# Two layers in one TensorE-bound kernel: gains of the key and first query weights applied in place, and another order of the last steps

## The chip, the cores and the metric

The kernel runs on one core of one Trainium2 chip. The metric is the device time of one execution in microseconds (us), the median over several runs. The engines are named as in the profile: PE is TensorE's matmul, PEld its weight load, DVE is VectorE, ACT is ScalarE, POOL is GpSimd, and SP issues most transfers.

## The reference

One step of an encoder with two layers on 1024 prompt rows and 32 rows of a running stream (1056 columns in all), width 1024. The first layer is a gated linear recurrence, the second an attention over a window of key and value rows that are computed once between the layers. All of it is float32.

```python
def shared_kv(h, norm_kv, w_kv, pos):
    kv = rmsnorm(h, norm_kv) @ w_kv
    k = rope(kv[..., :kvw].reshape(B, T, N_KV_HEADS, HEAD_DIM), pos)
    v = kv[..., kvw:].reshape(B, T, N_KV_HEADS, HEAD_DIM)
...
def swa_block(x, pos, norm_pre, w_in, sinks, w_out, norm_post, k, v, attend):
    u = rmsnorm(x, norm_pre) @ w_in
    q = rope(u[..., :qw].reshape(B, T, N_HEADS, HEAD_DIM), pos)
    o = attend(q, k, v, sinks)
    y = (o * jax.nn.silu(u[..., qw:])) @ w_out
    return x + rmsnorm(y, norm_post)
```

`rmsnorm(x, g)` is x / sqrt(mean(x^2) + 1e-6) * g.

## The kernel before

Each float32 product is three matmuls: both factors are split into a high part (`hi`, rounded to the format that TensorE reads) and a low part (`lo`, the rest), and hi*hi, hi*lo and lo*hi are summed (`mm3`, `mm3_steps`). Weights come in half tiles of 128 rows by 4 x 128 columns (`weights`, L135): a load into `raw`, the gain of the norm, and the split into `whi` and `wlo`. The pools behind these names are rings: `raw` has four slots, `whi` and `wlo` six each, and a load or a write waits until a slot is free. The raw tiles of kA lie in a pool of their own with two slots (L141). For most second-layer weights POOL multiplies the gain into `raw` (L147), ACT copies it to `hi` (L128) and DVE subtracts (L129). For the names in `GAIN_ACT` (kA, kB, qA0, qB0: the two halves of the key weights and of the first query weights) the gain is taken up in the split itself, column block by column block (`split_scaled`, L131 to L133): four scaled copies on ACT and four scale-and-subtract steps on DVE for each half tile.

The rest around them: the value weights (`prep_v`, L849) also go through `split_scaled`, but the change leaves them as they are. Between the layers lies what is called the seam here. For each of three column blocks n of 384, 384 and 288 columns, the first layer's output is normed and added to the input (`post_norm`, L660 and L666), split to `xh` and `xl`, squared on ACT (L673, tile `qx`), summed on POOL (L675) and reduced by a matmul with a matrix of ones (L188, tile `ss_x`). The key matmuls rAk and rBk, the value matmuls vc (L167 to L169) and their transposition (L839, after a scaling on DVE, L827) run between these steps. `raw_g` names the gate weights of the second layer, which follow the first query weights in the ring.

The order in which each engine takes its instructions is not written down by hand. A scheduler goes through the whole program with its own estimates of durations and takes, on each engine, the ready instruction with the highest rank. The rank is the place in the program; `urgent()` moves it ahead by 300 places, and `pin` keeps an instruction behind those that precede it in the program. On the chip, each engine and each queue then works strictly in that order.

At the end (`out_t`, L1169) the last 256 prompt rows are computed with rows on the partitions: two tiles t of 128 rows, two halves c of 512 columns. ACT squares a finished bank and sums it along the row (L1200), DVE multiplies it by the gain (L1203) into `zt`. When both halves of a tile are there, 1/sqrt is taken from ACT's approximation y and refined once by r = y * (1.5 - 0.5 * m * y * y), with m the mean square; then z * r plus the residual (L1215) goes out in two stores of 512 columns (L1216). The last half of the last tile is computed in two parts of 256 columns, each with its own sum (s2 and s1).

Of the kernel before, what the change touches and what calls it, by code (L numbers as in the profile page):

```python
# [11 lines left out]
AF = mybir.ActivationFunctionType  # L12
ALU = mybir.AluOpType
# [62 lines left out]
def _trunk(ctx, tc, nc, A):  # L76
    V, S, G = nc.vector, nc.scalar, nc.gpsimd
# [10 lines left out]
    def urgent(offset=300):  # L88
        return tc.high_priority(offset=offset)

    def pin(i, on=True):
        return tc.keep_in_program_order(i) if on else i

    def bank(name, tag="mm", bufs=None):
        return psum.tile([P, 512], F32, tag=tag, name=name, bufs=bufs or nbank)
# [24 lines left out]
    def g_of(which, k):  # L120
        return gains[:, which * KD + k:which * KD + k + 1]


    def split(dst_hi, dst_lo, src, lo_eng=None, hi_dve=False, behind=False):
        if hi_dve:
            V.tensor_copy(dst_hi, src)
        else:
            pin(S.activation(dst_hi, src, AF.Copy), behind)  # L128
        (lo_eng or V).tensor_tensor(dst_lo, src, dst_hi.bitcast(F32), op=ALU.subtract)  # L129

    def split_scaled(dst_hi, dst_lo, src, gain, behind=False):  # L131
        pin(S.activation(dst_hi, src, AF.Copy, scale=gain), behind)
        V.scalar_tensor_tensor(dst_lo, src, gain, dst_hi.bitcast(F32), op0=ALU.mult, op1=ALU.subtract)  # L133

    def weights(src, kn, name, gain=None):  # L135

        out = []
        for k0 in range(0, kn, 4):
            kk = min(4, kn - k0)
            if name == "kA":  # L140
                raw = late.tile([P, 4, P], F32, tag="raw", bufs=2, name=f"raw_{name}_{k0}")  # L141
            else:
                raw = ring.tile([P, 4, P], F32, tag="raw", bufs=4, name=f"raw_{name}_{k0}")
            nc.sync.dma_start(raw[:, :kk, :], src[:, k0:k0 + kk, :])
            if gain is not None and name not in GAIN_ACT:
                with urgent():
                    pin(G.tensor_tensor(raw[:, :kk, :], raw[:, :kk, :],  # L147
                                        gains[:, gain * KD + k0:gain * KD + k0 + kk].unsqueeze(2).to_broadcast([P, kk, P]),
                                        op=ALU.mult), name in ("qA1", "qB1"))
            hi = ring.tile([P, 4, P], F32R, tag="whi", bufs=6, name=f"whi_{name}_{k0}")  # L150
            lo = ring.tile([P, 4, P], F32R, tag="wlo", bufs=6, name=f"wlo_{name}_{k0}")
            with urgent():
                if name in GAIN_ACT:
                    for i in range(kk):
                        split_scaled(hi[:, i, :], lo[:, i, :], raw[:, i, :], g_of(gain, k0 + i))
                else:
                    split(hi[:, :kk, :], lo[:, :kk, :], raw[:, :kk, :], G if name in LO_POOL else None, name in HI_DVE)
            out += [(hi[:, i, :], lo[:, i, :]) for i in range(kk)]
        return out
# [468 lines left out]
    def tmp(name, w=384):  # L628
        return late.tile([P, 384], F32, tag="t", bufs=NT, name=name)[:, :w]
# [81 lines left out]
    for n, order in enumerate(orders):  # L711
        zs, acc = {}, []
        w = NSB[n][1] - NSB[n][0]
        for i, m in enumerate(order):
# [5 lines left out]
            ps = bank(f"oa{m}_{n}")[:, :w]  # L720
            mm3(ps, [ws[k] for k in korder], [yhl[k, n] for k in korder])
            z = tmp(f"z{m}_{n}") if n < 2 else late.tile([P, 288], F32, tag="z", bufs=KD, name=f"z{m}_{n}")
# [30 lines left out]
    def mm3_steps(ps, ws, xs, every=6):  # L753
        n, c = len(ws), 0
        for i, ((wh, wl), (xh, xl)) in enumerate(zip(ws, xs)):
            for l, r in ((wh, xh), (wh, xl), (wl, xh)):
                nc.tensor.matmul(ps, l, r, start=c == 0, stop=c == 3 * n - 1)  # L757
                c += 1
                if c % every == 0 and c < 3 * n:
                    yield  # L760
# [311 lines left out]
    def load_og(m, n):  # L1072
        w = width(OUT[n])
        oghl[m, n] = (part(f"ogh{m}_{n}", w), part(f"ogl{m}_{n}", w))
        if m < 6:
            raw = unit(f"ogr{m}_{n}", w=w)
            load_parts(raw, ogscr[m], OUT[n])
            split(*oghl[m, n], raw)
            return
        o = 0  # L1080
        for c0, c1 in OUT[n]:
            i = min(c0 // 384, 2)
            split(*(x[:, o:o + c1 - c0] for x in oghl[m, n]), ogl[m, i][:, c0 - NSB[i][0]:c1 - NSB[i][0]], behind=n == 2 and m == 6)
            o += c1 - c0
# [69 lines left out]
    def fin_tile(name, w, tag, dt=F32, bufs=1):  # L1154
        return fin.tile([P, w], dt, tag=tag, bufs=bufs, name=name)[:, :w]

    def prep_t(c, k):

        raw = ring.tile([P, 4, P], F32, tag="raw", bufs=4, name=f"raw_t{c}_{k}").rearrange("p a b -> p (a b)")
        nc.sync.dma_start(raw, A["w_out_t"][c, k])  # L1160
        if c and k < 6:
            wt[c, k] = tuple(ring.tile([P, 4, P], F32R, tag=f"w{x}", bufs=6, name=f"wt{x}{c}_{k}").rearrange("p a b -> p (a b)")
                             for x in ("hi", "lo"))
        else:
            wt[c, k] = tuple(fin_tile(f"wt{x}{c}_{k}", 512, "wt" + x, F32R, 10) for x in "hl")

        split(*wt[c, k], raw, behind=c == 1)

    def out_t():  # L1169

        gpost = fin_tile("gpost", 1024, "gpost", bufs=1)
        nc.sync.dma_start(gpost, A["gpost"])
        x1t = fin.tile([P, KD, 256], F32, name="x1t")
        nc.sync.dma_start(x1t, x1scr.rearrange("m p c -> p m c")[:, :, 768:SEQ])
        sm = fin.tile([P, 2, 8], F32, name="smt")
        for m in range(KD):
            if (m, 2) not in oghl:
                load_og(m, 2)
        for k in (6, 7, 0, 1, 2, 3, 4, 5):
            prep_t(1, k)  # L1180
        zt = [fin_tile(f"zt{t}", 1024, "zt", bufs=2) for t in range(2)]
        xt = {}

        def residual(t):
            for c in range(2):
                xt[t, c] = bank(f"xt{t}_{c}", "ST"[t], 2)
                for i in range(4):
                    nc.tensor.transpose(xt[t, c][:, i * P:(i + 1) * P], x1t[:, 4 * c + i, t * P:(t + 1) * P], ident)

        for c in range(2):  # L1190
            for t in range(2):
                s0, s1, ms, y, r, s2 = (sm[:, t, i:i + 1] for i in range(6))

                parts = [(0, 256, s2), (256, 512, s1)] if c and t else [(0, 512, s1 if c else s0)]
                for a, b, acc in parts:
                    ps = bank(f"ot{t}_{c}_{a}")[:, :b - a]
                    yield from mm3_steps(ps, [tuple(x[:, t * P:(t + 1) * P] for x in oghl[k, 2]) for k in range(KD)],
                                         [tuple(x[:, a:b] for x in wt[c, k]) for k in range(KD)])
                    junk = fin_tile(f"junk{t}_{c}_{a}", b - a, "junk", bufs=1)
                    S.activation(junk, ps, AF.Square, accum_out=acc)  # L1200
                    if c == 0:
                        V.tensor_scalar(s0, s0, 1.0 / 1024.0, EPS, op0=ALU.mult, op1=ALU.add)
                    V.tensor_tensor(zt[t][:, c * 512 + a:c * 512 + b], ps, gpost[:, c * 512 + a:c * 512 + b], op=ALU.mult)  # L1203
                    if acc is s2:
                        V.scalar_tensor_tensor(s0, s2, 1.0 / 1024.0, s0, op0=ALU.mult, op1=ALU.add)
                if c == 1:
                    residual(t)
                    S.activation(y, s1, AF.Abs_reciprocal_sqrt, bias=s0, scale=1.0 / 1024.0)
                    V.tensor_scalar(ms, s1, 1.0 / 1024.0, s0, op0=ALU.mult, op1=ALU.add)
                    V.tensor_scalar(ms, ms, y, y, op0=ALU.mult, op1=ALU.mult)  # L1210
                    V.tensor_scalar(ms, ms, -0.5, 1.5, op0=ALU.mult, op1=ALU.add)
                    V.tensor_tensor(r, ms, y, op=ALU.mult)
                    for i in range(2):
                        z = zt[t][:, i * 512:(i + 1) * 512]
                        V.scalar_tensor_tensor(z, z, r, xt[t, i], op0=ALU.mult, op1=ALU.add)  # L1215
                        (nc.scalar if i else nc.sync).dma_start(A["o_yt"][t][:, i * 512:(i + 1) * 512], z)  # L1216
                yield

    nb = norm_b(0)
# [7 lines left out]
    for i, _ in enumerate(out_t()):  # L1227
        if i:
            next(nb, None)
# [90 lines left out]
```

## Time and profile before

| | |
|---|---|
| median of 3 runs | 898.28 us (897.15 to 898.77) |
| the profiled execution | 896.39 us, its span 894.6 us |
| PE busy in the span | 881.0 us (98%) |
| DVE busy | 702.3 us (79%) |
| ACT busy | 563.6 us (63%) |
| POOL busy | 211.5 us (24%) |

The span runs from the first to the last instruction of the profiled execution; its own time is 1.8 us longer. All times in rows are counted from the span's start. In rows of a timeline the first number is the start, the second the length; "x4" marks four instructions merged into one row; brackets give the idle time of the engine just before it and what ended it. Names such as `wlo_qA<-raw_qA` give the output and the inputs, and buffer numbers are left out.

### The profile page before, as it was taken

Reading aid. Unit: us, or ns where it says so; the run is one execution under the profiler, and the core shown is the slowest. Engines: PE = TensorE matmul, PEld = TensorE weight load, DVE = VectorE, ACT = ScalarE, POOL = GpSimd, SP = SyncE. Lnnn points to the kernel's source line nnn. Section 1 sums busy time; section 2 is a strip of 40 time slices with the busy share of each in tenths; the row PEclk is TensorE's granted clock in tenths of the full one; section 3 lists DMA queues with packets and bytes.
Section 4 is the critical chain, followed back from the end, with each engine's and each line's share of the span. In section 5 each row is a group of like instructions: output and inputs, shape, how many; then the busy total and the mean of one; then the engine's idle time right before and its main releaser. Section 6 shows DMA issues by size and latency. Waiting matters only on the chain.

```text
span 894.6 us, 15865 instructions
## 1 busy us (share of the span) xinstructions
PE 881.0 (98%) x5462; PEld 863.1 (96%) x5462; DVE 702.3 (79%) x1511; ACT 563.6 (63%) x1233; POOL 211.5 (24%) x257
## 2 busy tenths in 40 slices
PE   9999999999999999999998999999999999999996
PEld 8999999999999999999997999999999999999996
DVE  5877878879897654176889847879999999898777
ACT  7848878789354325355675317756767767797652
POOL 5260212134300001124343532113023011002240
PEclk9999999999999999999999999999999999999999
DMA  9533433352544226446455568336448338444984
GB/s 335 199 107 108 118 100 120 110 147 86 182 128 126 91 55 209 136 133 202 145 171 175 190 183 231 97 101 192 115 125 228 99 120 233 118 135 123 300 259 170
DMA packets 96129, 138.76 MB, mean 155 GB/s; under 512 B 16224, under 2 KB 64128, under 8 KB 96048
## 3 DMA queue, kind: packets, MB, share of 16 engines
q1 hardware_dynamic: 86232, 124.24, 45.6%
q10 hardware_dynamic: 9640, 12.96, 4.8%
q8 instruction: 43, 0.70, 0.3%
q0 software_dynamic: 176, 0.54, 0.2%
q14 instruction: 38, 0.31, 0.1%
HBM read 99.54 MB, written 32.13 MB: 147 GB/s over the span
## 4 chain that ended last, share of the span: by engine, by line
PE 66%; DVE 4%; ACT 2%; DMA 2%; issue 1%; POOL 1%; SPq 0%; DVEq 0%; ACTq 0%; POOLq 0%
PE gB L757 10%; PE rAq L757 5%; PE rBq L757 5%; PE obm L757 5%; PE oa L168 5%; PE oa L167 5%; PE oa L169 5%; PE gb L167 4%; PE gb L168 4%; PE gb L169 4%; PE S L984 3%; PE O L1019 3%; PE T L1009 3%; PE ot L757 2%; PE rAk L757 1%
## 5 line engine op out<-in xcount | busy, mean ns | idle before, releaser
L167 PE MATMUL oa<-yh,whi_outa 128*128 128x384 f32 (+1 forms) x264 | 85.8, 326 | 0.0
L168 PE MATMUL gb<-xlo,whi_ina 128*128 128x384 f32 (+1 forms) x264 | 85.6, 324 | 0.0
L167 PE MATMUL gb<-xhi,whi_ina 128*128 128x384 f32 (+1 forms) x264 | 85.3, 323 | 0.1
L169 PE MATMUL gb<-xhi,wlo_ina 128*128 128x384 f32 (+1 forms) x264 | 85.4, 323 | 0.0
L169 PE MATMUL oa<-yh,wlo_outa 128*128 128x384 f32 (+1 forms) x264 | 85.2, 323 | 0.0
L168 PE MATMUL oa<-yl,whi_outa 128*128 128x384 f32 (+1 forms) x264 | 85.1, 323 | 0.0
L675 POOL TENSOR_TENSOR qp<-qp,qp 128x384 f32<-128x384 f32 (+2 forms) x34 | 42.2, 1242 | 178.5 <-ACT qp L673 166.4
L168 PE MATMUL br<-xlo,whi_ina 128*128 128x384 f32 (+1 forms) x240 | 77.7, 324 | 0.0
L167 PE MATMUL br<-xhi,whi_ina 128*128 128x384 f32 (+1 forms) x240 | 77.7, 324 | 0.0
L169 PE MATMUL br<-xhi,wlo_ina 128*128 128x384 f32 (+1 forms) x240 | 77.5, 323 | 0.0
L129 DVE TENSOR_TENSOR wlo_outa<-raw_outa,whi_outa 128x512 fp32r<-128x512 f32 (+1 forms) x60 | 43.0, 731 | 43.1 <-ACT whi_outa L128 42.9
L989 ACT ACTIVATE P<-P,sm 128x257 f32<-128x257 f32 (+1 forms) x132 | 64.3, 489 | 13.1 <-DVE sm L986 12.8
L757 PE MATMUL gB<-xl,whi_g 128*128 128x384 f32 (+1 forms) x192 | 63.1, 329 | 0.0
L757 PE MATMUL gB<-xh,whi_g 128*128 128x384 f32 (+1 forms) x192 | 63.1, 329 | 0.0
L128 ACT ACTIVATE whi_outa<-raw_outa 128x512 fp32r<-128x512 f32 (+1 forms) x60 | 35.5, 594 | 43.4 <-PE oa L168 23.9
L757 PE MATMUL gB<-xh,wlo_g 128*128 128x384 f32 (+1 forms) x192 | 62.8, 327 | 0.0
L986 DVE CUSTOM_DVE_ANT_0 P<-S,mask,nsnk 128x256 f32<-128x256 f32 (+1 forms) x128 | 53.1, 461 | 5.5 <-PE S L984 5.4
L257 DVE SCALAR_TENSOR_TENSOR conv<-ext,pa,conv 128x1060 f32<-128x1060 f32 (+2 forms) x51 | 46.1, 926 | 11.0 <-ACT conv L255 10.5
L167 PEld LDWEIGHTS gb<-xhi,whi_ina 128*128 128x128 f32 x264 | 49.7, 188 | 0.4 <-DVE u L565 0.4
L167 PEld LDWEIGHTS oa<-yh,whi_outa 128*128 128x128 f32 x264 | 49.6, 188 | 0.4
L168 PEld LDWEIGHTS oa<-yl,whi_outa 128*128 128x128 f32 x264 | 49.6, 188 | 0.4
L169 PEld LDWEIGHTS oa<-yh,wlo_outa 128*128 128x128 f32 x264 | 49.7, 188 | 0.0
(316 smaller groups left out, 2889.4 us busy)
## 6 DMA issues: line engine op xcount, KB each, us to landing
raw_ina<-w_in_a SPq DMA_DIRECT2D x44, 256.0 KB, 3.6
raw_outa<-w_out_a SPq DMA_DIRECT2D x40, 256.0 KB, 3.1
raw_ob<-w_out_b SPq DMA_DIRECT2D x32, 256.0 KB, 3.2
qscr<-quadq SPq DMA_DIRECT2D x8, 768.0 KB
Q<-qscr SPq DMA_DIRECT2D x32, 192.0 KB, 3.8
hscr<-u SPq DMA_DIRECT2D x11, 530.0 KB, 2.7
xr<-xr SPq DMA_DIRECT2D x8, 512.0 KB, 8.9
raw_g<-w_in_b SPq DMA_DIRECT2D x16, 256.0 KB, 5.2
```

Of the source, the lines that this page charges most:

```text
L128: pin(S.activation(dst_hi, src, AF.Copy), behind)
L129: (lo_eng or V).tensor_tensor(dst_lo, src, dst_hi.bitcast(F32), op=ALU.subtract)
L167: pin(nc.tensor.matmul(ps, wh, xh, start=i == 0, stop=False), behind and i == 0 or mid and i == n // 2)
L168: nc.tensor.matmul(ps, wh, xl, start=False, stop=False)
L169: nc.tensor.matmul(ps, wl, xh, start=False, stop=last and i == n - 1)
L257: V.scalar_tensor_tensor(c, e[:, c0 + k:c1 + k], pa[:, t, k:k + 1], c, op0=ALU.mult, op1=ALU.add)
L675: G.tensor_tensor(sums[0], sums[0], q, op=ALU.add)
L757: nc.tensor.matmul(ps, l, r, start=c == 0, stop=c == 3 * n - 1)
L984: pin(nc.tensor.matmul(s, q, KU[g, n][:, hl, ks], start=hl == 0, stop=hl == 1), g == 0 and j == 0)
L986: V.tensor_tensor_reduce(pt[:, h, :w], sb[:, (h - h0) * 256:(h - h0) * 256 + w], msk, -0.125, nsnk[:, sk][:, h:h + 1], op0=ALU.add, op1=AL ...
L989: S.activation(pt[:, h, :w + 1], pt[:, h, :w + 1], AF.Exp, bias=nmax[:, h:h + 1], scale=-1.0, accum_out=rsum[:, h:h + 1])
L1009: nc.tensor.transpose(tb[:, h * P:(h + 1) * P], st["P"][:, h, kt * P:(kt + 1) * P], ident)
```

## The change

For the four weights in `GAIN_ACT`, ACT now multiplies the gain into `raw` in place, four column blocks one by one, and the half tile is then split whole: one copy on ACT, one subtraction on DVE. In `out_t` the refinement is regrouped as r = 1.5 y + (-0.5 m) y * y, so that one small step on DVE goes away, 1.5 y is computed on ACT, and -0.5 times the part of m that is known earlier (s2h) is prepared ahead. The approximation y and the step for m now stand ahead of the last gain multiplication, which is pinned behind them. The last tile's second half is finished and stored in two pieces of 256 columns instead of one of 512; the issue alternates between SP and ACT.

```diff
                 if name in GAIN_ACT:
                     for i in range(kk):
-                        split_scaled(hi[:, i, :], lo[:, i, :], raw[:, i, :], g_of(gain, k0 + i))
+                        S.activation(raw[:, i, :], raw[:, i, :], AF.Copy, scale=g_of(gain, k0 + i))
+                    split(hi[:, :kk, :], lo[:, :kk, :], raw[:, :kk, :])
...
-                s0, s1, ms, y, r, s2 = (sm[:, t, i:i + 1] for i in range(6))
+                s0, s1, ms, y, r, s2, s2h = (sm[:, t, i:i + 1] for i in range(7))
...
-                    V.tensor_tensor(zt[t][:, c * 512 + a:c * 512 + b], ps, gpost[:, c * 512 + a:c * 512 + b], op=ALU.mult)
+                    if acc is s1:
+                        S.activation(y, s1, AF.Abs_reciprocal_sqrt, bias=s0, scale=1.0 / 1024.0)
+                        V.tensor_scalar(ms, s1, -0.5 / 1024.0, s2h, op0=ALU.mult, op1=ALU.add)
+                        S.activation(r, y, AF.Copy, scale=1.5)
+                    pin(V.tensor_tensor(zt[t][:, c * 512 + a:c * 512 + b], ps, gpost[:, c * 512 + a:c * 512 + b], op=ALU.mult), acc is s1)
                     if acc is s2:
                         V.scalar_tensor_tensor(s0, s2, 1.0 / 1024.0, s0, op0=ALU.mult, op1=ALU.add)
+                    if acc is s2 or c == 0:
+                        V.tensor_scalar(s2h, s0, -0.5, None, op0=ALU.mult)
                 if c == 1:
                     residual(t)
-                    S.activation(y, s1, AF.Abs_reciprocal_sqrt, bias=s0, scale=1.0 / 1024.0)
-                    V.tensor_scalar(ms, s1, 1.0 / 1024.0, s0, op0=ALU.mult, op1=ALU.add)
                     V.tensor_scalar(ms, ms, y, y, op0=ALU.mult, op1=ALU.mult)
-                    V.tensor_scalar(ms, ms, -0.5, 1.5, op0=ALU.mult, op1=ALU.add)
-                    V.tensor_tensor(r, ms, y, op=ALU.mult)
-                    for i in range(2):
-                        z = zt[t][:, i * 512:(i + 1) * 512]
-                        V.scalar_tensor_tensor(z, z, r, xt[t, i], op0=ALU.mult, op1=ALU.add)
-                        (nc.scalar if i else nc.sync).dma_start(A["o_yt"][t][:, i * 512:(i + 1) * 512], z)
+                    V.scalar_tensor_tensor(r, ms, y, r, op0=ALU.mult, op1=ALU.add)
+                    for i, (a, b) in enumerate(((0, 512), (512, 768), (768, 1024)) if t else ((0, 512), (512, 1024))):
+                        z = zt[t][:, a:b]
+                        V.scalar_tensor_tensor(z, z, r, xt[t, a // 512][:, a % 512:a % 512 + b - a], op0=ALU.mult, op1=ALU.add)
+                        (nc.scalar if i % 2 else nc.sync).dma_start(A["o_yt"][t][:, a:b], z)
```

## The prediction

> **What bounds the kernel now.** I read the page first (span, engines), then PE's waits, the busy time by stretches around the longest wait, the timeline of each engine there, and at last the chain that ended last.
>
> ```profile
> span 894.6 us, 15865 instructions
> PE 881.0 (98%) x5462; PEld 863.1 (96%) x5462; DVE 702.3 (79%) x1511; ACT 563.6 (63%) x1233; POOL 211.5 (24%) x257
> ```
>
> TensorE is busy 881.0 of 894.6 us, so 13.6 us are not covered by it. The change removes no matmul; it can only touch that remainder and the slow clock behind a pause. Two places matter: the seam between the two layers (460 to 490 us), where the key and first query weights are split, and the end.
>
> ```profile
> 460.00:475.00 15.00, 14.31 (x76) 12.90 (x75) 11.81 (x35) 12.55 (x38) 1.83 (x2) 1.00 0.52 153
> 475.00:480.00 5.00, 4.65 (x25) 4.32 (x25) 4.67 (x11) 0.94 (x2) 0.65 (x1) 1.00 0.88 270
> 480.00:483.00 3.00, 0.05 (x1) 0.05 (x1) 3.00 (x3) 0.00 (x0) 2.90 (x3) 1.00 0.52 121
> 483.00:487.00 4.00, 4.00 (x12) 3.40 (x13) 4.00 (x12) 2.91 (x8) 0.00 (x0) 0.57 0.80 225
> ```
>
> Columns: length, PE, PEld, DVE, ACT, POOL, granted clock, DMA share, GB/s. PE stands still for 0.69 + 0.35 + 2.95 = 4.0 us in the seam, and then four microseconds run at a granted clock of 0.57. VectorE is full from 480 to 487. Who ends the pause:
>
> ```profile
> 472.49 1.26 ACT L132 ACTIVATE whi_qA<-raw_qA,gains 128x128 fp32r<-128x128 f32 x4
> 473.42 1.13 DVE L133 SCALAR_TENSOR_TENSOR wlo_qA<-raw_qA,gains,whi_qA 128x128 fp32r<-128x128 f32 x4
> 474.58 0.87 SPq L144 DMA_DIRECT2D raw_g<-w_in_b  x2
> 474.87 0.55 DVE L660 TENSOR_TENSOR z<-z,r 128x384 f32<-128x384 f32 x1
> 476.47 0.51 ACT L673 ACTIVATE qx<-z 128x384 f32<-128x384 f32 x1
> 479.35 2.38 POOL L147 TENSOR_TENSOR raw_g<-raw_g,gains 128x512 f32<-128x512 f32 x2 [7.26 <-DMA res<-xT]
> 481.69 1.20 POOL L675 TENSOR_TENSOR qx<-qx,qx 128x384 f32<-128x384 f32 x1
> 482.95 1.50 PE L188 MATMUL ss_x<-qx,ones 128*128 128x384 f32 x2 [3.30 <-POOL qx L675]
> ```
>
> The wait of 3.30 us is on GpSimd's sum of squares (L675). Its input qx is there at 476.98, but two gain multiplications of raw_g stand ahead of it on POOL. They start when raw_g lands; raw_g is issued at 474.58, and the last wlo_qA ends at 473.42 + 1.13 = 474.55. So I read the slot of raw_g as freed by the query split: **when the query's lower halves end decides when PE goes on.**
>
> **The change, part by part. Weights.** Eight half tiles (kA, kB, qA0, qB0, two each) of 128x512. Durations in ns (min/median/max):
>
> ```profile
> L132 ACT ACTIVATE whi_kA<-raw_kA,gains x8: 386/388/399, 456.5 to 461.6; 128x128 fp32r<-128x128 f32 x8
> L133 DVE SCALAR_TENSOR_TENSOR wlo_kA<-raw_kA,gains,whi_kA x8: 340/343/1102, 458.1 to 462.1; 128x128 fp32r<-128x128 f32 x8
> L128 ACT ACTIVATE whi_qA<-raw_qA x6: 616/628/635, 539.5 to 676.6; 128x512 fp32r<-128x512 f32 x6
> L129 DVE TENSOR_TENSOR wlo_qA<-raw_qA,whi_qA x6: 675/688/1227, 540.2 to 679.3; 128x512 fp32r<-128x512 f32 x6
> L144 SPq DMA_DIRECT2D raw_kA<-w_k x2: 426/428/430, 331.1 to 331.6; - x2
> ```
>
> Each half now takes four scales on ACT (taken at the 388 ns of the scaled copy of the same shape), one whole copy (628) and one subtraction on DVE (688). ACT gains one copy per half: 0.63 us, of which about 0.1 overlaps its neighbour (four copies of 388 take 1.27 in the rows, not 1.55), so 0.53; over eight halves +4.2 us. DVE gives back 1.13 - 0.69 = 0.44 per half, 3.5 us in all.
>
> What counts is where the scales stand. Before, the scaled copy writes a whi slot (six of them, freed by matmuls). After, it writes raw itself and needs only raw. raw_kA was issued at 331.6, yet its first reader comes at 456.48, so something other than its data holds it, and the slot is the likeliest. Rows of the next stretch:
>
> ```profile
> 456.48 1.27 ACT L132 ACTIVATE whi_kA<-raw_kA,gains 128x128 fp32r<-128x128 f32 x4
> 460.32 0.51 ACT L132 ACTIVATE wh_v<-raw_v,gains 128x256 fp32r<-128x256 f32 x1 [2.57 <-DMA raw_v<-wv]
> 460.73 1.27 ACT L132 ACTIVATE whi_kA<-raw_kA,gains 128x128 fp32r<-128x128 f32 x4
> 462.02 0.34 PE L757 MATMUL rAk<-xh,whi_kA 128*128 128x384 f32 x1
> 465.38 1.12 DVE L133 SCALAR_TENSOR_TENSOR wlo_kB<-raw_kB,gains,whi_kB 128x128 fp32r<-128x128 f32 x4
> 466.53 0.80 SPq L144 DMA_DIRECT2D raw_qA<-w_in_b  x2
> 470.18 0.40 ACT L132 ACTIVATE whi_qA<-raw_qA,gains 128x128 fp32r<-128x128 f32 x1 [1.67 <-DMA raw_qA<-w_in_b]
> ```
>
> ACT idles 2.57 us ahead of 460.32, in which the scales of kB fit (8 x 0.29 = 2.3), and those of kA can go far earlier. I take it that the scheduler places them so. Then each half past 460 costs ACT 0.53 instead of 1.17: for kA's second half and both of kB 3 x 0.64 = 1.9 us less. kB's last lower half ends 1.9 sooner, at 464.6, and raw_qA is issued right behind it (466.53 against 466.50 now) and arrives 1.9 sooner, since 470.18 is a wait for that load. PE's demand at 462.02 is met: the copy of kA's second half starts at 460.72 and ends at 461.35.
>
> The query halves hide nothing, because ACT waits for their load: the first half's copy adds 0.53 and the second's copy and subtraction together 0.5 over the present 0.80 from last copy to last subtraction. I take +0.9 (DVE, lighter, returns 0.1). So raw_g goes out 1.9 - 0.9 = 1.0 us sooner, and L147, L675 and ss_x with it: **-1.0 us**. Bounds: 0, if the scales gain nothing on ACT; -1.9, if the query's extra work hides too. The load of qB0 also meets lighter splits, but its splits stand at 504 us with PE covered; I cost them at nothing, and 2 x 0.53 of ACT time if that cover is gone.
>
> Does the pause's end carry through? PE next needs VectorE here:
>
> ```profile
> 488.68 1.01 DVE L827 TENSOR_TENSOR vc<-vc,r 128x384 f32<-128x384 f32 x2
> 489.49 0.27 PE L839 MATMUL v<-ident,vc 128*128 128x128 f32 x1
> ```
>
> The first vc is ready near 489.2, 0.3 ahead of its transposition. DVE must therefore move up too. Its full stretch begins with L660 at 474.87, right behind the query and value splits, and moves with them by the same 1.0.
>
> **The end.** The last chain, engine by engine:
>
> ```profile
> 888.24 0.19 ACT L1200 ACTIVATION_READ_ACCUMULATOR junk<-ot 128x1 f32 x1
> 888.46 0.42 DVE L1203 TENSOR_TENSOR zt<-ot,gpost 128x256 f32<-128x256 f32 x1 [0.18 <-ACT junk L1200]
> 888.80 0.20 DVE L1209 TENSOR_SCALAR smt<-smt 128x1 f32<-128x1 f32 x1
> 889.11 0.27 DVE L1210 TENSOR_SCALAR smt<-smt 128x1 f32<-128x1 f32 x1
> 889.42 0.15 DVE L1211 TENSOR_SCALAR smt<-smt 128x1 f32<-128x1 f32 x1
> 889.61 0.16 DVE L1212 TENSOR_TENSOR smt<-smt 128x1 f32<-128x1 f32 x1
> 889.87 1.40 DVE L1215 SCALAR_TENSOR_TENSOR zt<-zt,smt,xt 128x512 f32<-128x512 f32 x2
> 890.64 0.33 SPq L1216 DMA_DIRECT2D o_yt<-zt  x1
> 891.50:891.75 0.25, 0.00 (x0) 0.00 (x0) 0.00 (x0) 0.00 (x0) 0.00 (x0) 1.00 0.98 369
> 892.75:893.00 0.25, 0.00 (x0) 0.00 (x0) 0.00 (x0) 0.00 (x0) 0.00 (x0) 0.50 0.52 189
> ```
>
> After: L1209's successor goes first (888.46), zt 0.12 later (888.58), the two squarings by y 0.34 later (888.92, y long there), the last small step 0.31 later (889.23), L1215 0.26 later: 889.49 instead of 889.87, **-0.4 us**. The 1.5 y on ACT runs beside zt. The second half of the row becomes two pieces: half of 1.40, then two 256-wide steps at L1203's pace (0.34 to the next, 0.42 to its end) make 1.46, about as now. The stores run at full DMA share from before 891.5 until 892.9 (512 KB at 369 GB/s is 1.4 us), so they end when the first starts plus 1.4: smaller last stores give nothing of their own. The bounds are 0 (pieces of 1 KB a row move slower and eat it) and -0.7 (the last store's issue counted). The added s2h step (0.15) and the third issue lie off the chain.
>
> Sum: -1.0 - 0.4 = -1.4 us, on the profiled execution's 896.39 us, which is 1.9 under the median of the runs; put on the median it makes 898.28 - 1.4 = 896.9. The short PE waits before 475 (0.69 us) gain nothing, because the pause behind them ends when POOL is done.
>
> **The rivals.** First, the clock. In the 4 us at 0.57, (1 - 0.57) x 4 = 1.7 us were lost after a pause of 3.3. A shorter pause may not bring the clock down. PE would then be 1.7 ahead, but vc on DVE leaves it only the 0.3 us: 896.6. Against it: value matmuls end sooner as well, so the pause may stay near 3. The Trainium skill, TensorE: Matmul & The Clock Gate, "HAM oscillation — how this bites in real kernels", warns of PE gaps over about 3.4 us; the trace agrees about in size, 3.3 us, and by this rule any shortening would keep the clock.
>
> Second, POOL takes qx ahead of raw_g, since qx comes sooner and raw_g's splits stretch. Then DVE decides:
>
> ```profile
> 478.06 5.52 DVE L660 TENSOR_TENSOR z<-z,r 128x288 f32<-128x288 f32 x8
> 483.50 1.92 DVE L666 TENSOR_TENSOR z<-z,res 128x288 f32<-128x288 f32 x5
> ```
>
> Eight at 1.92/5 = 0.38 would be 3.1 us, but took 5.5 while POOL multiplied raw_g. Without that overlap DVE gains up to 2.4 more; I take 1.8: 896.9 - 1.8 = 895.1.
>
> Third, the other side: the scales are not placed ahead but stay where the scaled copies stand. Then kA's second half and both of kB cost 0.53 more each (+1.6), and the query +1.0: raw_g 2.6 later, PE too, less 0.4 at the end: +2.2, 900.5. It decides if the scales of kB stand behind 460.32 on ACT. For it speaks that the scheduler works by its own times, against it the free raw_kA and the 2.57 us.
>
> Fourth, and rarer, scaling qB0 in place as soon as it lands puts a wait for a load ahead of the norm's steps in ACT's queue; up to 3 us if its load lands that much behind them: near 900.
>
> **How the numbers follow.** Main case 0.48 (895.8 to 898.2), clock 0.13, POOL order 0.16, scales not ahead 0.13, qB0 in the way 0.06, anything else 0.04 (both sides). About 0.2% (1.8 us) is what a measurement of this kernel can tell from no change; the main case ends just inside that line, so a quarter of it counts as faster, with half of the clock case and all of the POOL case: 0.12 + 0.07 + 0.16 and an allowance of 0.05 for deeper placement, 0.40; slower 0.13 + 0.06 and 0.01, 0.20; the same 0.40. The range 894.0 to 900.2 leaves out the far end of the POOL case and about half of the slow ones.
>
> **What would show it.** Right: eight scales of kA well ahead of 456 us, kB's ahead of the first wh_v, whole copies of 0.63 behind; raw_qA issued near 464.6; raw_g near 473.6; ss_x near 482; the last tile's first residual step 1.25 us behind the start of its accumulator read (888.24) instead of 1.63. Wrong: scales standing beside the copies at 460 to 467, PE waiting in rAk or rBk, another order on POOL, or a new pause past 490 us from a different plan.

## The result and the profile after

The changed kernel needs 904.49 us (median of 5 runs, 903.28 to 907.07), the kernel before 898.77 (5 runs, 897.15 to 900.01). The ratio is 1.008, 95% interval 1.0061 to 1.010: it is slower by 0.8%, where 896.9 with a range of 894.0 to 900.2 was forecast. The profiled execution of the changed kernel took 904.49 us with a span of 902.7; that of the kernel before had 894.6. From L156 on, line numbers are one higher than before. The page's first lines:

```profile
span 902.7 us, 15871 instructions
PE 884.2 (98%) x5462; PEld 865.3 (96%) x5462; DVE 700.5 (78%) x1489; ACT 569.0 (63%) x1243; POOL 215.4 (24%) x257
```

The same 5462 matmuls keep PE busy for 3.2 us more (884.2 against 881.0), and the span is 8.1 longer. So some matmuls ran slower, and there is about 5 us of new idle time. PE's waits (us in total, times, longest):

```profile
PE v L840 <- DVE vc L828: 4.5, 1, 4.5
PE vc L168 <- ACT wh_v L132: 1.9, 2, 1.2
...
PE rAq L758 <- DVE vc L828: 0.8, 1, 0.8
...
PE ss_x L189 <- POOL qx L676: 0.3, 1, 0.3
```

The pause ahead of ss_x went from 3.3 to 0.3 us, but only because PE comes there later: it has waited 1.9 us for the value weights (wh_v), and behind these waits, of 1.21 and 0.72 us, the granted clock falls to 0.50 for about three microseconds. The row below is the stretch 475 to 480 (length, PE, PEld, DVE, ACT, POOL, clock, DMA share, GB/s; before, the clock was 1.00 there):

```profile
475.00:480.00 5.00, 4.17 (x15) 3.68 (x15) 3.84 (x9) 4.17 (x12) 0.81 (x1) 0.73 0.79 229
```

A pause of 4.5 us now stands where there was none, ahead of the first transposition of v, and VectorE ends it. The first rows below are the first v transposition and the first obm matmul (of the second layer's output) after; the last is obm before, whose v transposition stood at 489.49:

```profile
L840 PE MATMUL v<-ident,vc x18: 270/272/476, 492.8 to 547.0; 128*128 128x128 f32 x16, 128*32 128x128 f32 x2
L758 PE MATMUL obm<-ogh,whi_ob x128: 331/347/650, 788.4 to 870.5; 128*128 128x384 f32 x64, 128*128 128x416 f32 x64
```

```profile
L757 PE MATMUL obm<-ogh,whi_ob x128: 331/348/650, 781.4 to 862.4; 128*128 128x384 f32 x64, 128*128 128x416 f32 x64
```

At the transposition the changed kernel is 3.3 us behind (0.6 of it already at the first key matmul, 460.5 against 459.9), at obm 7.0: the way between them took 295.6 us instead of 291.9. There are two losses to explain, 3.3 up to the transposition and 3.7 behind it. (The other 1.1 come behind the start of obm. From there to the end the profiles of kernels with the new end scatter between 112.8 us in k_pin_tail and 115.3 in fill_own_bank, both below; before it was 113.2, after 114.3. So they are not laid to the change.) ScalarE (start, duration, idle time ahead and what ended it):

```profile
469.57 1.28 ACT L155 ACTIVATE raw_qA<-raw_qA,gains 128x128 f32<-128x128 f32 x4 [1.66 <-DMA raw_qA<-w_in_b]
470.75 0.49 ACT L128 ACTIVATE quadck<-ck 128x128 fp32r<-128x128 f32 x2
471.15 0.49 ACT L132 ACTIVATE wh_v<-raw_v,gains 128x256 fp32r<-128x256 f32 x1
...
475.31 0.99 ACT L155 ACTIVATE raw_qB<-raw_qB,gains 128x128 f32<-128x128 f32 x3 [0.33 <-DMA raw_qB<-w_in_b]
476.20 0.49 ACT L132 ACTIVATE wh_v<-raw_v,gains 128x256 fp32r<-128x256 f32 x1
476.60 0.39 ACT L155 ACTIVATE raw_qB<-raw_qB,gains 128x128 f32<-128x128 f32 x1
476.90 0.48 ACT L192 ACTIVATE y_p<-ss_p,epst 128x288 f32<-128x288 f32 x1
477.85 0.98 ACT L155 ACTIVATE raw_qB<-raw_qB,gains 128x128 f32<-128x128 f32 x3 [0.47 <-DMA raw_qB<-w_in_b]
...
479.44 0.51 ACT L674 ACTIVATE qx<-z 128x384 f32<-128x384 f32 x1
```

The scales of both query halves wait for their loads in the middle of the queue. Behind them stand a value weight, the norm's y_p and the square qx, which came at 476.47 before and comes at 479.44 now. VectorE follows:

```profile
476.73 0.49 DVE L133 SCALAR_TENSOR_TENSOR wl_v<-raw_v,gains,wh_v 128x256 fp32r<-128x256 f32 x1 [0.94 <-ACT wh_v L132]
477.13 0.55 DVE L661 TENSOR_TENSOR z<-z,r 128x384 f32<-128x384 f32 x1
...
480.62 4.69 DVE L661 TENSOR_TENSOR z<-z,r 128x288 f32<-128x288 f32 x8
...
487.81 0.54 DVE L193 SCALAR_TENSOR_TENSOR t_x<-ss_x,y_x 128x384 f32<-128x384 f32 x1
488.65 0.54 DVE L194 SCALAR_TENSOR_TENSOR t_x<-t_x,y_x 128x384 f32<-128x384 f32 x1
489.49 0.54 DVE L195 SCALAR_TENSOR_TENSOR r<-t_x,y_x 128x384 f32<-128x384 f32 x1
490.32 0.54 DVE L775 TENSOR_TENSOR rp0k<-rAk,cos 128x384 f32<-128x384 f32 x1
492.19 1.00 DVE L828 TENSOR_TENSOR vc<-vc,r 128x384 f32<-128x384 f32 x2
```

Two things are to be seen. The full stretch starts 2.26 us later (477.13 against 474.87). And three steps of the next norm's reciprocal root (t_x, t_x, r) now stand ahead of the key's rotation and of vc, for which PE waits; before, t_x stood behind vc. Last, the granted clock. The row is the stretch 491.0 to 497.5, first after, then before:

```profile
491.00:497.50 6.50, 4.72 (x15) 4.72 (x16) 6.50 (x10) 3.65 (x10) 6.34 (x8) 0.50 0.09 34
```

```profile
491.00:497.50 6.50, 6.50 (x40) 6.43 (x40) 6.50 (x9) 2.54 (x7) 4.64 (x5) 1.00 0.13 45
```

At the end of the long pause and behind it the clock is at half for 6.5 us; 1.8 us of them still belong to the pause. PE gets 15 matmuls done there, not 40.

### The profile page after: what moved, and what is told of

Its sections match the earlier page's. It is cut to its first block, busy times and chain, and to the rows that moved or that the text cites. A ratio compares the mean times of both kernels' runs of the same rounds, so it can differ in the third digit from the quotient of the medians.

```text
span 902.7 us, 15871 instructions
## 1 busy us (share of the span) xinstructions
PE 884.2 (98%) x5462; PEld 865.3 (96%) x5462; DVE 700.5 (78%) x1489; ACT 569.0 (63%) x1243; POOL 215.4 (24%) x257
## 5 line engine op out<-in xcount | busy, mean ns | idle before, releaser
L676 POOL TENSOR_TENSOR qp<-qp,qp 128x384 f32<-128x384 f32 (+2 forms) x34 | 46.6, 1370 | 174.4 <-ACT qp L674 162.3
```

The costliest lines, as they stand in the source:

```text
L676: G.tensor_tensor(sums[0], sums[0], q, op=ALU.add)
```

## The experiments

Three theories. **A**: scales that need only raw stand early in ScalarE's queue and wait there for their load, in front of work that DVE needs; qB0 above all. **B**: the order on VectorE, t_x ahead of vc. **C**: the clock after the new pause. The rivals are that the whole splits themselves or the new end cost the time. All results in one table; "v" is the start of the first v transposition, "key to v" the time from the first key matmul to it (before 29.6, after 32.3), and "to obm" the time from v to the first obm matmul (before 291.9, after 295.6), each from the kernel's one profile. That profile is one run and need not be the median one: f2_rsqrt_pinned's took 902.02 us, the longest of its seven runs, and kqa_without_qB0's 899.53, 1.3 under its median. Kernels reach the seam up to 2 us apart, so "key to v" compares better than v. The ratio is to the kernel before, run on the same chip beside it (medians 897.39 to 898.15 us).

| run | median us | ratio (95%) | v | key to v | to obm |
|---|---|---|---|---|---|
| seam | 903.91 | 1.0064 (1.0052 to 1.0076) | 492.4 | 31.8 | 295.9 |
| tail | 897.65 | 0.9999 (0.9988 to 1.0010) | 491.5 | 29.7 | 291.8 |
| f2_rsqrt_pinned | 900.87 | 1.0032 (1.0021 to 1.0042) | 490.5 | 30.8 | 294.9 |
| kqa_without_qB0 | 900.79 | 1.0035 (1.0020 to 1.0050) | 490.8 | 30.9 | 293.6 |
| noqb_pin | 897.61 | 0.9997 (0.9985 to 1.0010) | 489.4 | 29.8 | 291.9 |
| fill_pause | 907.56 | 1.0103 (1.0081 to 1.0125) | 499.3 | 31.9 | 292.9 |
| fill_own_bank | 901.90 | 1.0038 (1.0025 to 1.0052) | 492.7 | 32.7 | 292.0 |
| qb_alone | 898.49 | 1.0010 (0.9995 to 1.0025) | 490.8 | 30.1 | 292.1 |
| qa_alone | 901.93 | 1.0041 (1.0026 to 1.0055) | 491.0 | 31.3 | 295.9 |
| k_alone | 897.34 | 0.9991 (0.9976 to 1.0006) | 490.5 | 28.7 | 291.9 |
| k_pin_tail | 896.64 | 0.9986 (0.9973 to 0.9998) | 488.4 | 28.6 | 292.4 |
| k_pin_tail_term | 896.59 | 0.9979 (0.9968 to 0.9990) | 488.7 | 28.0 | 292.0 |

**Which half of the change.** seam takes only the first hunk of the diff, tail only the second (L1190 on).

> The kernel before with the edit of the weight splits alone (key and first query weights scaled in place and split whole); its end is as before. In the changed kernel obm begins 7.0 us later than before and the tail takes 0.1 us less. Theory A (the scales wait for their loads in ACT's queue ahead of wh_v2_1, wh_v3_1, y_p and qx, so DVE's full stretch starts 2.26 us later) and theory B (three rsqrt steps t_x stand ahead of rope and vc on DVE, so the first v transposition comes 3.3 us later and vc n=1 5.6 us later) both expect the whole loss here: 904 to 906 us, obm 7 us late. The rival that the tail's edit costs the time expects 898 to 900.

> The kernel before with the edit of the end alone (shorter chain, three stores). Theories A and B: the time stays within 0.5 us of the kernel before, 0.1 to 0.4 us under it (the tail of the changed kernel took 6.26 instead of 6.36 us from the accumulator read to the end). The rival that the tail costs the time: 902 or more.

seam has nearly the whole loss (6.0 us over the kernel before), tail none. The end is out.

**One cause at a time.** f2_rsqrt_pinned is the changed kernel with DVE's old order at this place:

```
-        V.scalar_tensor_tensor(t, ps[:, :n], EPS, y, op0=ALU.add, op1=ALU.mult)
+        pin(V.scalar_tensor_tensor(t, ps[:, :n], EPS, y, ...), nm == "x1_1")
```

> The changed kernel, but the first DVE step of the rsqrt of x1_1 is held in program order, so that the three steps t_x (1.65 us) stand behind vc on DVE again. Theory A alone: DVE's full stretch still starts near 477.1 and the time is little better, 903 to 904.5. Theory B: vc L828 comes 1.7 us earlier, the pause ahead of the first v transposition is 2.8 instead of 4.5 us, and the clock after it falls less (0.59 to 0.72 in the changed kernel), so 900.5 to 902.5. The rival that the whole split's own ACT time costs it: no change, 904.5.

kqa_without_qB0 leaves qB0 out instead:

```
-                if name in GAIN_ACT:
+                if name in ('kA', 'kB', 'qA0'):
                     ... scaled in place, split whole
+                elif name in GAIN_ACT:
+                    ... split_scaled as before
```

> The kernel before with kA, kB and qA0 scaled in place and split whole, but qB0 as before; the end as before. On DVE the steps t_x still stand ahead of vc. Theory A, with qB0 as its main part: ACT reaches wh_v3_1, y_p and qx about 2 us earlier than in the changed kernel and DVE's full stretch starts near 475, so 900 to 902 us. Theory B alone: t_x still ahead, so still 903 to 905 us.

Each gets back about half: 900.87 and 900.79. First f2_rsqrt_pinned, then kqa_without_qB0, on DVE:

```profile
479.74 4.69 DVE L661 TENSOR_TENSOR z<-z,r 128x288 f32<-128x288 f32 x8
...
489.91 1.00 DVE L828 TENSOR_TENSOR vc<-vc,r 128x384 f32<-128x384 f32 x2
```

```profile
477.78 5.52 DVE L664 TENSOR_TENSOR z<-z,r 128x288 f32<-128x288 f32 x8
...
490.17 1.01 DVE L831 TENSOR_TENSOR vc<-vc,r 128x384 f32<-128x384 f32 x2
```

With qB0 in place, DVE's eight multiplications start 1.7 us later than before (478.06); with t_x ahead they start in time, but vc (488.68 before) is 1.5 us late all the same. Neither theory is enough alone. In these two profiles the clock behind the transposition differs: it is 0.50 from 490 to 496 in f2_rsqrt_pinned, behind a pause of 3.46 us, and stays at 1.00 in kqa_without_qB0, behind one of 3.38. So the 1.7 us by which kqa_without_qB0's way to obm is too long are not the clock's; 1.2 of them are a wait of PE at 519 us for a later vc.

**Both undone.** noqb_pin is f2_rsqrt_pinned with qB0 as before, so it differs from each of the two above in one cause (from kqa_without_qB0 in the end as well).

> The changed kernel with both causes undone: qB0 as before, and the first DVE step of the rsqrt of x1_1 held in program order; kA, kB and qA0 stay in place and whole, the new end stays. Theories A and B together: the two shares, 3.6 (904.5 to 900.9) each when undone alone, do not add up fully, but nearly the whole loss of 6.2 is gone, 897.5 to 899. If a third cause in kA, kB or qA0 (the scales of qA0 wait 1.8 us for their load ahead of quadck and wh_v2_1) is worth 1 us or more: 899 to 900.5.

897.61 us: the loss is gone. So the four make a square: neither cause 897.6, qB0 alone on top 900.9 (+3.3), the t_x order alone on top 900.8 (+3.2), both 903.9 to 904.5 (+6.3 to 6.9). The two add up. This settles the place of the loss. The second share is the price of the order with what hangs on it: the r of these steps also scales the tables cos and sin on POOL. In kqa_without_qB0 POOL takes them at 488.46 and 489.43, ahead of the key's rotation (rp0k, 490.38); in noqb_pin rp0k stands first, at 488.13, and cos comes at 498.07. How much of the 3.2 us is POOL's was not tested apart. PE's waits in noqb_pin:

```profile
PE ss_x L192 <- POOL qx L679: 2.7, 1, 2.7
PE v L843 <- DVE vc L831: 1.6, 1, 1.6
```

**The clock.** 16 idle matmuls in the pause, first into the warm-up tile's bank (fill_pause), then into a bank of their own:

```
         ps = bank(f"v{t}")[:m, :256]
+        if t == 0:
+            fb = bank("fill")          # fill_pause: wps
+            for _ in range(16):
+                pin(nc.tensor.matmul(fb[:, :P], ones, ones, start=True, stop=True))
```

> The changed kernel with 16 extra 128x128 matmuls on PE (results unused) directly behind rAk and ahead of the first v transposition, in the stretch where PE otherwise waits 4.50 us for vc. Theory C (the pause takes the clock down: 0.50 from 491 to 497 in the changed kernel, where the matmuls follow each other every 0.32 instead of 0.17 us, so 4.8 us at half pace lose about 2.2): the clock stays at 1.00 and the time is 1.5 to 2.2 us under the changed kernel's, 902.3 to 903. Against it: what follows is bound by DVE, so PE's lost pace is hidden; then no change, 904.5.

> The changed kernel with 16 extra 128x128 matmuls on PE (results unused) behind rAk and ahead of the first v transposition, as in fill_pause, but into a PSUM bank of their own that is held only there. Theory C (the fall of the clock to 0.50 after the 4.50 us pause costs 2.2 us, since PE is behind from there on): the clock stays at 1.00 from 490 to 500, the way from the first v transposition to the first obm matmul is 293 instead of 295.6 us, and the time is 902 to 903. Against it: PE's lost pace is hidden behind DVE, then 904 to 905.

fill_pause came out slower, 907.56. It is a miss of the edit: already in the first layer, at 235 us, its PE waits 3.4 us for VectorE where the changed kernel doesn't, and it enters the seam some 7 us late. I read that as the warm-up tile now living until the fill at 494 us, so that one PSUM bank is missing all the way. Its way from v to obm did shrink. fill_own_bank has no such flaw (32 records are its 16 matmuls):

```profile
487.72 3.73 PE L842 MATMUL fill<-ones 128*128 128x128 f32 x32
492.73 0.33 PE L844 MATMUL v<-ident,vc 128*128 128x128 f32 x1 [1.27 <-DVE vc L828]
```

```profile
491.00:497.50 6.50, 5.23 (x34) 4.97 (x33) 6.50 (x10) 3.63 (x10) 6.34 (x8) 1.00 0.10 35
```

The transposition starts at the same time as in the changed kernel (492.73 against 492.78), nothing is done earlier, yet with the clock at 1.00 the way to obm is 292.0 us, as in the kernel before, and the median is 2.6 us lower. So in the changed kernel the loss behind the transposition (3.7 us in its profile, 2.6 in the medians) is the clock's and what follows from it. Theory C holds, with somewhat more than the 2.2 us expected. The earlier fall, at 475 to 480, is still there (0.70).

**One name at a time.** From the kernel before, only qB0, only qA0, or only kA and kB are taken into the new branch.

> The kernel before with qB0 alone scaled in place and split whole; on DVE the steps t_x stand behind vc as before. Theory A: its eight scales stand behind wh_v3_1 and ahead of y_p and qx on ACT and wait for their load, so DVE's full stretch starts 1 to 2.5 us later and the time is 898.9 to 900.5. Theory B alone: the order on DVE is as before, so 898 +- 0.7.

> The kernel before with qA0 alone scaled in place and split whole. On DVE the three steps t_x stand ahead of rope and vc. Theory B: this order costs about as much as it does between kqa_without_qB0 and noqb_pin (900.8 - 897.6 = 3.2 us): 899.5 to 901.5. Theory A alone (only qB0 costs): 897.4 +- 0.7.

> The kernel before with the key weights kA and kB alone scaled in place and split whole, the queries and the end as before; t_x stands behind vc. Theories A and B: no scale waits for a load ahead of the norm's steps and DVE's order is as before, so no loss: 896.4 to 898.3, with up to 1.9 us of the ACT time that the key halves give back. The rival that whole splits in themselves cost time: 899 or more.

qb_alone: its median is 1.1 us above, and the interval takes in no change. The wait is there, y_p is late and DVE with it, as its timeline of VectorE shows:

```profile
477.82 0.46 DVE L196 SCALAR_TENSOR_TENSOR t_p<-ss_p,y_p 128x288 f32<-128x288 f32 x1 [1.60 <-ACT y_p L195]
```

But PE still pauses for 3.1 us at ss_x and not at the transposition, and the way to obm is as before (292.1). The price of the same scales is not clear of none here (at most 2.2 us by the interval) and 3.3 us beside qA0. That it hangs on where PE's pause falls fits the profiles, but was not tested apart.

qa_alone costs more than theory B gave it (901.93, expected 899.5 to 901.5), and by its profile not in the way expected. Only the first of the three steps stands ahead of vc:

```profile
474.53 0.69 DVE L129 TENSOR_TENSOR wlo_qA<-raw_qA,whi_qA 128x512 fp32r<-128x512 f32 x1 [1.20 <-ACT whi_qA L128]
...
487.69 0.55 DVE L196 SCALAR_TENSOR_TENSOR t_x<-ss_x,y_x 128x384 f32<-128x384 f32 x1
```

What else delays it is the whole split itself: DVE waits 1.20 us for a copy that stands on ACT behind all eight scales of both halves (the last four start at 472.72 and take 1.26 us). PE's pause ahead of the transposition is 4.3 us, with the clock at half behind it. So qA0 alone brings part of the delay. With the keys in place as well the same subtraction starts at 473.21 instead of 474.53 (noqb_pin, where t_x is held back too), and nothing is lost. The changed order on DVE is seen only in kernels with qA0 in place (seam, the changed kernel, kqa_without_qB0, qa_alone), not in qb_alone or k_alone. Why the scheduler turns the order with it was not found out.

k_alone: no loss, 897.34 at 0.9991. The rival that whole splits in themselves cost time falls for the keys.

**A version that keeps what gains.** k_pin_tail takes the keys, the pin and the new end, with both queries as before; k_pin_tail_term besides gives the last square straight to PE:

```
-    TERMS = {"p1_2": (7,)}
+    TERMS = {"p1_2": (7,), "x1_1": (7,)}
```

> The kernel before with kA and kB scaled in place and split whole, the new end, and the rsqrt step of x1_1 held in program order; both query weights as before. k_alone needed 0.9 us less than the kernel before from the first rAk matmul to the first obm matmul (320.6 against 321.5), and the new end gives up to 0.2. Theory A and B: nothing that costs is left, so 0.5 to 1.2 us under the kernel before, 896.2 to 897. If the 0.9 us is chance of one profile: no change, 897.4.

> k_pin_tail, and besides the last square of block 1 goes to PE as a third term of ss_x instead of through POOL's addition (1.20 us, started behind raw_g's 2.4 us). PE's wait of 2.0 to 3.3 us ahead of ss_x goes. If that wait bounds this stretch: 1 to 2 us under k_pin_tail. If DVE's vc bounds it (ready 0.3 us ahead of the transposition in the kernel before), PE only waits at the transposition instead: within 0.7 us of k_pin_tail.

Both are faster than the kernel before, by 0.14% and 0.21%, with intervals that end at 0.9998, barely short of no change, and 0.9990. The second is faster than both kernels: 896.59 us against 904.49 and, beside it, 898.15. The third term itself does nothing that can be told (medians 0.05 us apart). PE's waits, first k_pin_tail, then k_pin_tail_term, which has none at ss_x:

```profile
PE v L843 <- DVE vc L831: 2.7, 1, 2.7
PE ss_x L192 <- POOL qx L679: 1.6, 1, 1.6
```

```profile
PE v L843 <- DVE vc L831: 3.1, 1, 3.1
```

The 1.6 us at ss_x are gone, 0.4 of them come back at the transposition, and 0.6 remain in "key to v" (28.0 for 28.6); the median shows none of it. What PE waits for last in this stretch is VectorE, not POOL.

## Why the prediction was wrong, point by point

**The keys: right.** kA's scales stand at 335 to 341 us and kB's ahead of the value weights, as forecast. In noqb_pin, which has all three weights up to qA0 in place, raw_qA goes out at 464.43; 464.6 was forecast. In the changed kernel, whose first key matmul starts 0.6 us later in its run, it goes out at 465.27.

**The query: the term was mis-sized.** +0.9 us was taken; from raw_qA's issue to raw_g's it was 8.05 us before (466.53 to 474.58), and in noqb_pin it is 10.50, so +2.45. The first scale starts 4.25 us behind the issue instead of 3.65 (+0.6), and from there to the end of the last subtraction it is 6.22 instead of 4.37 us (+1.85):

```profile
464.43 1.12 SPq L144 DMA_DIRECT2D raw_qA<-w_in_b  x2
...
474.93 0.80 SPq L144 DMA_DIRECT2D raw_g<-w_in_b  x2
```

I counted the busy time of the added copy, as if scale, copy and subtraction of a half ran in one go. In fact quadck, a value weight, qx and the second half's scales stand between the first scales and the first copy. The forecast of -1.0 us for raw_g was therefore +0.4 at best, and with qB0 in the way it went out at 475.82, +1.2. k_alone and k_pin_tail bear this out: without the queries the key's gain reaches PE ("key to v" 0.9 and 1.0 us shorter than before).

**qB0 "at nothing": this step failed.** I reasoned from where its splits stood, at 504 us. But a scaled copy needs a whi slot, while the in-place scale needs only raw: the scales went to 475 to 479 us, and the first whole copy of qB0, which still needs the slot, stands at 510.0. I used just this reason for kA and did not carry it on to qB0's place in the sum. It costs 3.3 us in this kernel (f2_rsqrt_pinned against noqb_pin). My fourth rival had the mechanism, the place and the price (up to 3 us, near 900; f2_rsqrt_pinned, where it stands without the t_x order, is at 900.87), at a chance of 0.06.

**"DVE must therefore move up too": this step failed as well.** I shifted VectorE's work as a block. Its order changed, and the margin of 0.3 us that I had quoted for vc was there to say how little was needed: three steps of 0.47 us from start to start ahead of vc are 1.4 us, and with what hangs on them they cost 3.2.

**The clock** I weighed only as a gain, a pause getting shorter. The pause moved to a place where PE has no slack behind it. The loss of 1.7 us behind the old pause was hidden in VectorE's time, as noqb_pin shows: no fall of the clock (1.00 from 470 to 500), and v at 489.4 all the same. Behind the new pause it counts: 2.6 us of the changed kernel's time. The Trainium skill, TensorE: Matmul & The Clock Gate, "HAM oscillation — how this bites in real kernels", warns of PE gaps over about 3.4 us. The traces agree with it above that length (0.50 behind 4.50, 4.3 and 3.46 us) and in part below (1.00 behind 3.38 in kqa_without_qB0 and 3.10 in k_pin_tail_term). But the clock also fell behind 3.30 us before, 3.11 in qb_alone and 1.95 in k_alone (0.50 from 485 to 487). So it does not hold that any shortening would keep the clock, as the first rival had it.

**The end: right in kind, too large.** -0.4 was forecast. From the last accumulator read to the end it was 894.6 - 888.24 = 6.36 us and is 902.7 - 896.44 = 6.26:

```profile
896.44 0.19 ACT L1201 ACTIVATION_READ_ACCUMULATOR junk<-ot 128x1 f32 x1
...
896.80 0.42 DVE L1208 TENSOR_TENSOR zt<-ot,gpost 128x256 f32<-128x256 f32 x1
897.13 0.27 DVE L1215 TENSOR_SCALAR smt<-smt 128x1 f32<-128x1 f32 x1
897.50 0.22 DVE L1216 SCALAR_TENSOR_TENSOR smt<-smt 128x1 f32<-128x1 f32 x1
897.82 1.53 DVE L1219 SCALAR_TENSOR_TENSOR zt<-zt,smt,xt 128x512 f32<-128x512 f32 x3
```

The residual starts 1.38 us behind the read instead of the forecast 1.25 (before: 1.63). Up to zt and the first small step the forecast holds (0.36 and 0.69 behind the read, 0.34 and 0.68 forecast); the last small step comes 0.07 later than forecast, and the residual another 0.06. The rest, three pieces of 1.53 instead of two of 1.40, eats 0.15. Smaller last stores gave nothing, as forecast.

In sum, -1.4 was forecast; measured are about +3.3 for qB0, +3.2 for the order on DVE with what hangs on it (the two include the 2.6 of the clock, in shares that are not known), and nothing that can be told for the keys, qA0 and the end together (noqb_pin, 0.9997).

## What to carry to other kernels

When an edit frees an instruction from a resource (here the whi slot), the scheduler can place it earlier, and on an engine that works in order it then waits for its next resource (here the load) in front of everything behind it. Ask this for each instruction the edit touches, not only for those that it is meant to help. Where two engines stand 0.3 us apart, price the order on the second one too; and ask of a pause not only how long it is, but whether the engine has slack behind it, since the slow clock that may follow is free in one place and costs 2.6 us in another.

## What the runs showed of the hardware

Matmuls with no use, put into a pause of 4.5 us, made the kernel 2.6 us faster without moving anything that it waits for (904.49 to 901.90): the granted clock stayed at 1.00 where it had been 0.50 for 6.5 us. The length of a single pause does not tell the clock alone: k_pin_tail_term, with 3.1 us ahead of the transposition, kept 1.00 from 470 to 500, while qb_alone, also with 3.1 us, but ahead of ss_x, fell:

```profile
485.00:490.00 5.00, 5.00 (x21) 5.00 (x21) 5.00 (x14) 3.85 (x10) 0.51 (x1) 0.64 0.63 207
```

A fall needs no long pause either. In the changed kernel PE waits 1.21 and 0.72 us between 473 and 477, is busy for half of that stretch, and the clock is at 0.50 from 478 to 480. The kernels seam, f2_rsqrt_pinned, kqa_without_qB0, qa_alone and fill_own_bank show such a fall too (0.66 to 0.70 in the mean from 475 to 480). The kernel noqb_pin, with much the same waits (its longest is 1.12), does not: 1.00. What decides stays open. In kqa_without_qB0 this early fall cost nothing up to ss_x, since PE still waited 0.8 us for POOL there.
